# Attention scores with three persistent 32 KB buffers, and the second unit's transposes placed beside the third and fourth output tiles

## The chip, the cores and the metric

One core of a Trainium2 chip runs the kernel. The metric is the device time of one execution in microseconds; the runs of one kernel in one set of rounds lie within 0.1 to 0.5% of each other. A profiled execution gives the profile and the trace; its span (201.3 us for the kernel before) is about 1.8 us shorter than the device time.

## The reference

```python
batch, heads, seq, dim = 8, 8, 512, 64          # q, k: float32, 8.4 MB each
scale = 1.0 / np.sqrt(q.shape[-1])
return (np.einsum('bhqd,bhkd->bhqk', q, k) * scale).astype(np.float32)   # 67.1 MB
```

Two inputs are read once (16.8 MB together) and 67.1 MB are written: 83.9 MB cross the DMA engines whatever the order of work.

## The kernel before

The work is cut into 4 units of two batches. A unit is loaded as one 32 KB-per-partition tile (keys, then queries), cast to bf16 by POOL, transposed 128x128 at a time on PE, and copied out of PSUM into `kT` and `qz`. Then 4 output tiles of 4.19 MB are made per unit: 8 evacuations of PSUM each, and one store. The same pool of three 32 KB buffers serves the loads and the output tiles.

```python
big_pool = ctx.enter_context(tc.tile_pool(name="big", bufs=3))
# ...
def evacuate(dst, src):
    nonlocal n_evac
    if n_evac % 6 in (0, 2, 3):
        pinned(nc.scalar.mul(out=dst, in_=src, mul=scale))
    else:
        pinned(nc.vector.tensor_scalar(out=dst, in0=src, scalar1=scale, ...))
    n_evac += 1
# ...
def load_and_cast(v):
    xf = big_pool.tile([P, 2, 2, J * D], f32, name="big")
    for x, src in enumerate((k_r, q_r)):
        nc.sync.dma_start(out=xf[:, x], in_=...)
    for x in range(2):
        xb = bf_pool.tile([P, J, 2, D], bf16, name="xb")
        for s in range(2):
            pinned(nc.gpsimd.tensor_copy(out=xb[:, :, s, :], in_=xf[:, x, s]...))
# ... transpose(v, kb, qb): a generator of 40 steps; 8 groups of 8 transposes,
#     each group with 4 copies out of PSUM, on DVE and ACT in turn
def scores(v, t):
    o = big_pool.tile([P, 2, RO, S], f32, name="big")
    # ... 8 times: 2 matmuls into ps, evacuate(o[...], ps), yield
    nc.sync.dma_start(out=out_r[v, t], in_=o...)
# ...
for _ in transpose(0, *cast[0]):
    pass
for v in range(UNITS):
    ahead = transpose(v + 1, *cast[v + 1]) if v + 1 < UNITS else iter(())
    for t in range(TILES):
        for n, _ in enumerate(scores(v, t)):
            take(ahead, 1 + (t > 0 if v == 0 else n % 4 == 3))
```

`cast` is filled for all 4 units before the loop, so the fourth load waits for the first buffer, the first output tile for the second, and so on in rotation.

Of the kernel before, what the change touches and what calls it, by code (L numbers as in the profile page):

```python
# [1 line left out]

# [5 lines left out]


@with_exitstack  # L10
def kernel(
    ctx: ExitStack,
    tc: tile.TileContext,
    q: bass.AP,
    k: bass.AP,
    out: bass.AP,
):






    nc = tc.nc
    B, H, S, D = q.shape
    scale = 1.0 / (D ** 0.5)
    P = 128
    UNITS = B // 2
    N = H
    M = P // (2 * H)  # L30
    R = S // M
    J = R // 2
    RO = 8
    U = S // RO
    JJ = J // RO
    IW = 8 // JJ
    TILES = N // 2

    f32 = mybir.dt.float32
    bf16 = mybir.dt.bfloat16  # L40

    q_r = q.rearrange("(v b) g (m j) d -> v (b g m) (j d)", b=2, j=R)
    k_r = k.rearrange("(v b) g (m j) d -> v (b g m) (j d)", b=2, j=R)
    out_r = out.rearrange("(v b) (t x h) (u i) k -> v (b t) (h u) x (i k)", b=2, x=2, h=2, i=RO)

    consts = ctx.enter_context(tc.tile_pool(name="consts", bufs=1))

    big_pool = ctx.enter_context(tc.tile_pool(name="big", bufs=3))
    bf_pool = ctx.enter_context(tc.tile_pool(name="bf", bufs=6))
    t_pool = ctx.enter_context(tc.tile_pool(name="t", bufs=2))  # L50
    tpsum_pool = ctx.enter_context(tc.tile_pool(name="tpsum", bufs=2, space=bass.MemoryType.PSUM))
    psum_pool = ctx.enter_context(tc.tile_pool(name="psum", bufs=3, space=bass.MemoryType.PSUM))


    pinned = tc.keep_in_program_order

    n_evac = 0
    n_tp = 0

    def evacuate(dst, src):  # L60
        nonlocal n_evac

        if n_evac % 6 in (0, 2, 3):
            pinned(nc.scalar.mul(out=dst, in_=src, mul=scale))  # L64
        else:
            pinned(nc.vector.tensor_scalar(out=dst, in0=src, scalar1=scale, scalar2=None,  # L66
                                           op0=mybir.AluOpType.mult))
        n_evac += 1

    def half(h):  # L70
        return slice(h * D, (h + 1) * D)

    def load_and_cast(v):

        xf = big_pool.tile([P, 2, 2, J * D], f32, name="big")
        both = []
        for x, src in enumerate((k_r, q_r)):
            nc.sync.dma_start(out=xf[:, x], in_=src[v].rearrange("p (s c) -> p s c", s=2))  # L78
        for x in range(2):
            xb = bf_pool.tile([P, J, 2, D], bf16, name="xb")  # L80
            for s in range(2):
                pinned(nc.gpsimd.tensor_copy(out=xb[:, :, s, :],  # L82
                                             in_=xf[:, x, s].rearrange("p (j d) -> p j d", j=J)))
            both.append(xb)
        return both

    def rearrange(tp, pattern, dst):

        nonlocal n_tp
        copy = (nc.vector.tensor_copy, nc.scalar.copy)[n_tp % 2]  # L90
        n_tp += 1
        for s in range(2):
            src = tp[half(s)].rearrange(pattern, n=N, h=2)
            for h in range(2):
                pinned(copy(out=dst(s, h), in_=src[:, h]))  # L95
                yield

    def transpose(v, kb, qb):


        kT = t_pool.tile([P, N, M, 2, J], bf16, name="kT")
        qz = qzs[v % 2]
        ts[v] = (kT, qz)
        for j0 in range(0, J, 8):
            tp = tpsum_pool.tile([P, 8, P], bf16, name="tp")
            for j in range(8):
                pinned(nc.tensor.transpose(out=tp[:, j, :], identity=identity,  # L107
                                           in_=kb[:, j0 + j].rearrange("p s d -> p (s d)")))
            yield
            yield from rearrange(tp, "d j (n h m) -> d h n m j",  # L110
                                 lambda s, h: kT[half(h), :, :, s, j0:j0 + 8])
        for i0 in range(0, RO, IW):
            tp = tpsum_pool.tile([P, IW, JJ, P], bf16, name="tp")
            for i in range(IW):
                for jj in range(JJ):
                    pinned(nc.tensor.transpose(out=tp[:, i, jj, :], identity=identity,  # L116
                                               in_=qb[:, RO * jj + i0 + i].rearrange("p s d -> p (s d)")))
            yield
            yield from rearrange(tp, "d i jj (n h m) -> d h i n m jj",
                                 lambda s, h: qz[half(h), i0:i0 + IW, :, h * U:(h + 1) * U]  # L120
                                 .rearrange("d i n (m s jj) -> d s i n m jj", s=2, jj=JJ)[:, s])

    def scores(v, t):

        kT, qz = ts[v]
        o = big_pool.tile([P, 2, RO, S], f32, name="big")
        for x in range(2):
            n = 2 * t + x
            for i in range(0, RO, 2):
                ps = psum_pool.tile([P, 2, S], f32, name="ps")  # L130
                for w in range(2):
                    pinned(nc.tensor.matmul(out=ps[:, w, :], lhsT=qz[:, i + w, n, :],  # L132
                                            rhs=kT[:, n].rearrange("d m s j -> d (m s j)"),
                                            start=True, stop=True))
                evacuate(o[:, x, i:i + 2, :], ps)
                yield
        nc.sync.dma_start(out=out_r[v, t], in_=o.rearrange("p x i k -> p x (i k)"))  # L137

    def take(steps, count):
        for _ in range(count):  # L140
            next(steps, None)

    identity = consts.tile([P, P], dtype=bf16)
    make_identity(nc, identity)
    qzs = [consts.tile([P, RO, N, P], bf16, name=f"qz{n}") for n in range(2)]
    for qz in qzs:
        nc.vector.memset(qz, 0.0)  # L147
    cast = [load_and_cast(v) for v in range(UNITS)]

    ts = {}  # L150
# [4 lines that stand above are left out]
        for t in range(TILES):  # L155
            for n, _ in enumerate(scores(v, t)):

                take(ahead, 1 + (t > 0 if v == 0 else n % 4 == 3))
        for _ in ahead:
            pass  # L160


# [1 line left out]
_INS = ['q', 'k']  # L164
_OUTS = [((8, 8, 512, 512), 'float32')]


# [23 lines left out]
```

## Time and profile before

| | kernel before |
|---|---|
| time, median of 3 (low to high) | 203.24 us (202.83 to 203.37) |
| span of the profiled run | 201.3 us |
| busy: DMA queue / DVE / ACT / PE / POOL | 98.1% / 63% / 50% / 49% / 15% |
| moved over the span | 417 GB/s |
| stores 1, 2, 3, 4 issued at | 38.2, 46.0, 58.3, 63.6 us |
| least time from a store's issue to its landing | 15.8 us |

How to read it: the DMA row of the page is the mean busy share of 16 DMA engines in each fortieth of the span. The stage table has one line for each stretch, with the busy time of each engine and, in its last two columns, the DMA share and GB/s. "To landing" is counted from the issue on SP's queue to the completion that other engines can wait for. The prediction shows these lines.

### The profile page before, as it was taken

Reading aid. Unit: us, or ns where it says so; the run is one execution under the profiler, and the core shown is the slowest. Engines: PE = TensorE matmul, PEld = TensorE weight load, DVE = VectorE, ACT = ScalarE, POOL = GpSimd, SP = SyncE. Lnnn points to the kernel's source line nnn. Section 1 sums busy time; section 2 is a strip of 40 time slices with the busy share of each in tenths; the row PEclk is TensorE's granted clock in tenths of the full one; section 3 lists DMA queues with packets and bytes.
Section 4 is the critical chain, followed back from the end, with each engine's and each line's share of the span. In section 5 each row is a group of like instructions: output and inputs, shape, how many; then the busy total and the mean of one; then the engine's idle time right before and its main releaser. Section 6 shows DMA issues by size and latency. Waiting matters only on the chain.

```text
span 201.3 us, 1456 instructions
## 1 busy us (share of the span) xinstructions
PE 99.2 (49%) x503; PEld 48.3 (24%) x512; DVE 126.4 (63%) x130; ACT 100.7 (50%) x129; POOL 30.6 (15%) x22
## 2 busy tenths in 40 slices
PE   0033366753976729463729554856535666710000
PEld 0033353321522414231315221432212222200000
DVE  6726659995989929796749796569635264530000
ACT  2016667786674856583837663856515341510000
POOL 1277777556000000000000000000000000000000
PEclk9999999998599996999975998888995857555555
DMA  6999999999999999999999999999999999999993
GB/s 205 430 443 430 420 433 440 420 407 427 433 436 425 422 443 427 430 423 440 430 423 433 433 430 427 440 430 423 433 436 430 410 446 433 420 423 433 433 427 163
DMA packets 5510, 83.97 MB, mean 417 GB/s; under 512 B 384, under 2 KB 384, under 8 KB 384
## 3 DMA queue, kind: packets, MB, share of 16 engines
q1 hardware_dynamic: 5504, 83.89, 98.1%
q8 instruction: 4, 0.07, 0.1%
q14 instruction: 2, 0.02, 0.0%
HBM read 16.78 MB, written 67.11 MB: 417 GB/s over the span
## 4 chain that ended last, share of the span: by engine, by line
DMA 63%; DVE 16%; PE 3%; POOL 3%; ACT 1%; POOLq 1%; issue 1%; SPq 0%; DVEq 0%; ACTq 0%
DMA out_dram<-big 43%; DMA big<-in_q_dram 20%; DVE big L66 12%; PE ps L132 3%; DVE qz L95 3%; POOL xb L82 3%; DVE kT L95 1%; ACT big L64 1%; POOLq L186 1%; SPq L78 0%; DVEq L66 0%; SPq L137 0%; ACTq L64 0%; POOLq L82 0%
## 5 line engine op out<-in xcount | busy, mean ns | idle before, releaser
L132 PE MATMUL ps<-kT,qz 128*128 128x512 bf16 x247 | 81.1, 450 | 55.1 <-ACT big L64 39.2
L66 DVE TENSOR_SCALAR big<-ps 128x1024 f32<-128x1024 f32 x64 | 76.3, 1222 | 39.9 <-DMA out_dram<-big 29.1
L64 ACT ACTIVATE big<-ps 128x1024 f32<-128x1024 f32 x64 | 63.7, 1023 | 57.0 <-DMA out_dram<-big 30.8
L132 PEld LDWEIGHTS <-qz 128*128 128x128 bf16 x256 | 27.5, 111 | 96.0 <-issue 83.2
L82 POOL CAST xb<-big 128x2048 bf16<-128x2048 f32 x16 | 29.9, 1896 | 17.6 <-DMA big<-in_k_dram 11.9
L95 DVE COPY kT<-tp 64x512 bf16<-64x512 bf16 x32 | 22.0, 687 | 6.3 <-PE tp L107 5.7
L95 ACT COPY kT<-tp 64x512 bf16<-64x512 bf16 x32 | 18.5, 578 | 14.7 <-PE tp L107 14.4
L95 DVE COPY qz<-tp 64x512 bf16<-64x512 bf16 x32 | 22.0, 687 | 3.1 <-PE tp L116 2.7
L95 ACT COPY qz<-tp 64x512 bf16<-64x512 bf16 x32 | 18.5, 578 | 3.9 <-PE tp L116 3.6
L107 PE MATMUL tp<-identity,xb 128*128 128x128 bf16 x128 | 12.0, 254 | 16.5 <-POOL xb L82 12.5
L116 PE MATMUL tp<-identity,xb 128*128 128x128 bf16 x128 | 12.8, 265 | 6.0 <-DVE kT L95 3.5
L107 PEld LDWEIGHTS <-xb 128*128 128x128 bf16 x128 | 10.5, 116 | 20.8 <-POOL xb L82 12.8
L116 PEld LDWEIGHTS <-xb 128*128 128x128 bf16 x128 | 11.3, 122 | 10.9 <-issue 8.9
L147 DVE MEMSET qz<- 128x4096 uint32 x2 | 6.9, 3472 | 2.5 <-PEq L175 1.7
L95 ACT ACT_TABLE_LOAD x1 | 1.3, 1283 | 0.7 <-PEq L175 0.7
masks.py:199 POOL TENSOR_SCALAR_AFFINE_SELECT identity<-identity 128x128 bf16<-128x128 bf16 x1 | 0.3, 294 | 0.1
masks.py:197 POOL MEMSET identity<- 128x128 bf16 x1 | 0.2, 205 | 0.3 <-POOLq L175 0.3
L175 POOL MEMSET const-float32-0.0<- 128x1 f32 x1 | 0.1, 99 | 0.2 <-issue 0.2
L175 POOL MEMSET const-bfloat16-1.0<- 128x1 bf16 x1 | 0.1, 102 | 0.0
L175 POOL MEMSET const-uint8-127<- 128x1 uint8 x1 | 0.1, 102 | 0.0
L175 POOL MEMSET const-float32-1.0<- 128x1 f32 x1 | 0.1, 99 | 0.0
## 6 DMA issues: line engine op xcount, KB each, us to landing
out_dram<-big SPq DMA_DIRECT2D x16, 4096.0 KB, 21.4
big<-in_k_dram SPq DMA_DIRECT2D x4, 2048.0 KB, 19.2
big<-in_q_dram SPq DMA_DIRECT2D x4, 2048.0 KB, 24.2
```

Source lines behind the costliest of these rows:

```text
L64: pinned(nc.scalar.mul(out=dst, in_=src, mul=scale))
L66: pinned(nc.vector.tensor_scalar(out=dst, in0=src, scalar1=scale, scalar2=None, op0=mybir.AluOpType.mult))
L82: pinned(nc.gpsimd.tensor_copy(out=xb[:, :, s, :], in_=xf[:, x, s].rearrange("p (j d) -> p j d", j=J)))
L95: pinned(copy(out=dst(s, h), in_=src[:, h]))
L107: pinned(nc.tensor.transpose(out=tp[:, j, :], identity=identity, in_=kb[:, j0 + j].rearrange("p s d -> p (s d)")))
L116: pinned(nc.tensor.transpose(out=tp[:, i, jj, :], identity=identity, in_=qb[:, RO * jj + i0 + i].rearrange("p s d -> p (s d)")))
L132: pinned(nc.tensor.matmul(out=ps[:, w, :], lhsT=qz[:, i + w, n, :], rhs=kT[:, n].rearrange("d m s j -> d (m s j)"), start=True, stop=True))
L147: nc.vector.memset(qz, 0.0)
L175: nc = _bacc.Bacc("TRN2", target_bir_lowering=False, num_devices=1)
L186: with _tile.TileContext(nc) as tc:
```

## The change

The intent is to get the first stores out earlier: buffers that never go back to a pool are waited for part by part (the third tile's first evacuation starts at 41.2 us in the changed kernel, after the first cast of the fourth keys, and at 48.8 in the kernel before, after the last cast of that load); the first unit's transposes use all PSUM buffers and its first cast is shared between DVE and POOL; and the second unit's transposes no longer slow the first two output tiles but go beside the third and fourth. ACT takes two thirds of the evacuations instead of half.

```diff
-    big_pool = ctx.enter_context(tc.tile_pool(name="big", bufs=3))
...
-        if n_evac % 6 in (0, 2, 3):
+        if n_evac % 3 < 2:
             pinned(nc.scalar.mul(out=dst, in_=src, mul=scale))
...
+    def next_big():
+        nonlocal n_big
+        n_big += 1
+        return bigs[(n_big - 1) % 3]
...
-        xf = big_pool.tile([P, 2, 2, J * D], f32, name="big")
+        xf = next_big().rearrange("p (x s c) -> p x s c", x=2, s=2)
...
-                pinned(nc.gpsimd.tensor_copy(out=xb[:, :, s, :], in_=...))
+                copy = nc.vector.tensor_copy if v == x == s == 0 else nc.gpsimd.tensor_copy
+                pinned(copy(out=xb[:, :, s, :], in_=...))
...
+            if v == 0 and n_tp % 4 > 1:
+                tp = psum_pool.tile([P, W, P], bf16, name="ps")
+            else:
+                tp = tpsum_pool.tile([P, W, P], bf16, name="tp")
...
-        o = big_pool.tile([P, 2, RO, S], f32, name="big")
+        o = next_big().rearrange("p (x i k) -> p x i k", x=2, i=RO)
...
+    bigs = [consts.tile([P, 2 * RO * S], f32, name=f"big{n}") for n in range(3)]
...
-                take(ahead, 1 + (t > 0 if v == 0 else n % 4 == 3))
+                take(ahead, (0, 0, 3, 2)[t] if v == 0 else 1 + (n % 4 == 3))
```

More of the change, by code (lines that the diff above doesn't have):

```diff
@@ L35 @@
     JJ = J // RO
-    IW = 8 // JJ
     TILES = N // 2
@@ L46 @@
     consts = ctx.enter_context(tc.tile_pool(name="consts", bufs=1))
-    big_pool = ctx.enter_context(tc.tile_pool(name="big", bufs=3))
     bf_pool = ctx.enter_context(tc.tile_pool(name="bf", bufs=6))
     t_pool = ctx.enter_context(tc.tile_pool(name="t", bufs=2))
+    psum_pool = ctx.enter_context(tc.tile_pool(name="psum", bufs=3, space=bass.MemoryType.PSUM))
     tpsum_pool = ctx.enter_context(tc.tile_pool(name="tpsum", bufs=2, space=bass.MemoryType.PSUM))
-    psum_pool = ctx.enter_context(tc.tile_pool(name="psum", bufs=3, space=bass.MemoryType.PSUM))
     pinned = tc.keep_in_program_order
@@ L71, in half @@
         return slice(h * D, (h + 1) * D)
+    n_big = 0
+    def next_big():
+        nonlocal n_big
+        n_big += 1
+        return bigs[(n_big - 1) % 3]
     def load_and_cast(v):
-        xf = big_pool.tile([P, 2, 2, J * D], f32, name="big")
+        xf = next_big().rearrange("p (x s c) -> p x s c", x=2, s=2)
         both = []
@@ L81, in load_and_cast @@
             for s in range(2):
-                pinned(nc.gpsimd.tensor_copy(out=xb[:, :, s, :],
-                                             in_=xf[:, x, s].rearrange("p (j d) -> p j d", j=J)))
+                copy = nc.vector.tensor_copy if v == x == s == 0 else nc.gpsimd.tensor_copy
+                pinned(copy(out=xb[:, :, s, :], in_=xf[:, x, s].rearrange("p (j d) -> p j d", j=J)))
             both.append(xb)
@@ L103, in transpose, with transposed @@
         ts[v] = (kT, qz)
-        for j0 in range(0, J, 8):
-            tp = tpsum_pool.tile([P, 8, P], bf16, name="tp")
-            for j in range(8):
-                pinned(nc.tensor.transpose(out=tp[:, j, :], identity=identity,
-                                           in_=kb[:, j0 + j].rearrange("p s d -> p (s d)")))
+        W = 8
+        def transposed(rows):
+            if v == 0 and n_tp % 4 > 1:
+                tp = psum_pool.tile([P, W, P], bf16, name="ps")
+            else:
+                tp = tpsum_pool.tile([P, W, P], bf16, name="tp")
+            for w, row in enumerate(rows):
+                pinned(nc.tensor.transpose(out=tp[:, w, :], identity=identity,
+                                           in_=row.rearrange("p s d -> p (s d)")))
+            return tp
+        for j0 in range(0, J, W):
+            tp = transposed([kb[:, j0 + j] for j in range(W)])
             yield
             yield from rearrange(tp, "d j (n h m) -> d h n m j",
-                                 lambda s, h: kT[half(h), :, :, s, j0:j0 + 8])
+                                 lambda s, h: kT[half(h), :, :, s, j0:j0 + W])
+        IW = W // JJ
         for i0 in range(0, RO, IW):
-            tp = tpsum_pool.tile([P, IW, JJ, P], bf16, name="tp")
-            for i in range(IW):
-                for jj in range(JJ):
-                    pinned(nc.tensor.transpose(out=tp[:, i, jj, :], identity=identity,
-                                               in_=qb[:, RO * jj + i0 + i].rearrange("p s d -> p (s d)")))
+            tp = transposed([qb[:, RO * jj + i0 + i] for i in range(IW) for jj in range(JJ)])
             yield
-            yield from rearrange(tp, "d i jj (n h m) -> d h i n m jj",
+            yield from rearrange(tp.rearrange("p (i jj) c -> p i jj c", jj=JJ),
+                                 "d i jj (n h m) -> d h i n m jj",
                                  lambda s, h: qz[half(h), i0:i0 + IW, :, h * U:(h + 1) * U]
```

## The prediction

DVE's busy time came to about 101 us with a term for the first cast; without the term it is 126 - 22 x 1.2 = 99.6 us.

> **What bounds the kernel now.** I read the page's slices and DMA queue first, then a table of the DMA engines by stage, then how long a store takes from issue to landing, then the chain of work that ended last. First the page: the first line is the mean busy share of the 16 DMA engines in 40 slices, the second what they moved, then the queue, its share of the 16 engines' span, and the bytes.
>
> ```profile
> DMA  6999999999999999999999999999999999999993
> GB/s 205 430 443 430 420 433 440 420 407 427 433 436 425 422 443 427 430 423 440 430 423 433 433 430 427 440 430 423 433 436 430 410 446 433 420 423 433 433 427 163
> ...
> q1 hardware_dynamic: 5504, 83.89, 98.1%
> ...
> HBM read 16.78 MB, written 67.11 MB: 417 GB/s over the span
> ```
>
> Only the first and last of 40 slices are not full. The queue's packets cover 98.1% of a span of 201.3 us, so all idle time of the DMA engines together is 1.9% of it, 3.8 us. No compute engine comes near (DVE 63%, ACT 50%, PE 49%). The same by stage; the last two columns are the DMA share and GB/s:
>
> ```profile
> 0.00:4.00 4.00, 0.00 (x0) 0.00 (x0) 2.34 (x1) 1.28 (x1) 0.70 (x6) 1.00 0.57 147
> 4.00:30.00 26.00, 8.69 (x74) 7.56 (x76) 15.62 (x18) 9.87 (x17) 16.68 (x9) 1.00 1.01 431
> 30.00:46.00 16.00, 10.69 (x74) 5.49 (x73) 15.13 (x17) 12.79 (x18) 10.40 (x7) 1.00 1.01 422
> 46.00:64.00 18.00, 12.09 (x58) 5.73 (x57) 14.95 (x17) 11.38 (x16) 2.80 (x2) 0.81 1.01 432
> 64.00:150.00 86.00, 50.86 (x262) 23.88 (x266) 64.05 (x68) 53.50 (x68) 0.00 (x0) 0.90 1.01 430
> 150.00:197.00 47.00, 16.91 (x41) 5.60 (x41) 14.33 (x12) 11.85 (x12) 0.00 (x0) 0.58 1.01 430
> 197.00:201.25 4.25, 0.00 (x0) 0.00 (x0) 0.00 (x0) 0.00 (x0) 0.00 (x0) 0.50 0.25 108
> ```
>
> From 4 to 197 us the share is 1.01 in every stage, that is, full, at 422 to 432 GB/s: the stage of loads alone, the one in which loads give way to stores, and the stage of stores. What is lost is lost in the first 4 us (0.57 full, before the queue has filled) and the last 4.25 us (0.25, the engines finishing one after another). The time is therefore 83.9 MB / 430 GB/s = 195.1 us plus about 6.2 us of ramp and tail.
>
> How near was the queue to running dry? Each of the 16 stores moves 4.19 MB, alone 4.19 / 430 = 9.75 us. From issue to landing they took:
>
> ```profile
> DMA to landing us min/median/max: 15.8/21.4/23.4
> ```
>
> Even the quickest took 15.8 us, so at least about 15.8 - 9.75 = 6 us of other traffic was ahead of it at its issue. The timeline names that quickest store, the third, and the evacuation into the same buffer that its landing released:
>
> ```profile
> 58.31 0.37 SPq L137 DMA_DIRECT2D out_dram<-big  x1
> ...
> 74.21 1.02 ACT L64 ACTIVATE big<-ps 128x1024 f32<-128x1024 f32 x1 [1.84 <-DMA out_dram<-big]
> ```
>
> 74.2 - 58.3 = 15.9 us. So the tightest place of the whole kernel, where the changed code works, still had 6 us in hand. The chain in order of time looks different at that very place:
>
> ```profile
> 45.07 1.90 POOL xb L82
> 46.96 1.85 POOLq L186
> 48.84 1.23 DVE big L66
> ...
> 60.06 3.50 DVE big L66 x3
> 63.61 20.21 DMA out_dram<-big
> ```
>
> It walks through casts, copies and evacuations from 45 to 63.6 us and reads as if compute set the end. But the 20.21 us behind it is longer than the store's own 9.75 us: the store queued. While those engines are named, the DMA engines are full, so shortening this stretch only lengthens the queue.
>
> [...] Here it is the engines: a store's issue takes 0.37 us of SP, 16 of them about 6 us of 201. [...]
>
> **The change part by part.** Bytes, number and shape of the DMAs, and rotation of three buffers in one order, all stay as they were. The order of instructions built from both versions shows the 8 loads and 16 stores equal, and 128 score evacuations, 64 + 64 transpose copies and 16 casts in both.
>
> Persistent buffers. Before, the first evacuation into a re-used buffer waits for all loads and casts of it; in the changed build it waits for the part that it overwrites (one load and its own cast for each half of a tile). Third tile: before, its first evacuation starts at 48.8 us, when the last cast of the fourth load ends. After, its first half needs only the casts of the fourth key load (39.09 + 3.74 = 42.8 us), its second half those that end at 48.8. Worth up to about 6 us to that tile, off the DMA path.
>
> First cast on VectorE. Two casts of 1.87 us stood in a row on POOL (8.71 to 12.4). Now one runs on DVE after the second memset (5.93 + 3.47 = 9.4 us)[...].
>
> Four PSUM buffers for the first 8 groups of transposes. PE no longer waits for copies (the 2.44 and 2.36 us gaps). But the queries land at 13.5 and their casts end at 17.3 as before. From there: about 1.1 us of transposes, then 8 DVE copies of 0.70 = 5.6 us, ends at 24.0; before, 29.0. A gain of 5 us, off the DMA path.
>
> Placement and split. The 40 steps of the next unit's transposes leave the first two tiles and go beside the third (24) and fourth (16). First tile: 8 evacuations, 6 on ACT at 1.03 = 6.2 us from 24 us, so its store goes out near 30 us, not 38.2. Second tile: its second half waits for casts that end at 33.15 + 3.74 = 36.9, so about 38.5, not 46.0. Third tile: about half of its 19 or 20 copies on each engine; ACT 5 x 1.03 + 10 x 0.58 = 11 us, DVE 3 x 1.23 + 10 x 0.69 = 10.6 us, between 42 and, with the cast that ends at 48.8, about 52 us, not 58.3. Fourth: waits for the first store's landing, near 53 us, then ACT 6 x 1.03 + 8 x 0.58 = 10.8 us: 64 us, as before (63.6).
>
> Is the queue ever dry? All loads and two stores are 25.2 MB, 58.5 us of DMA from an effective start near 3.2 us: full until 61.7. The third store arrives at 52, 10 us ahead (before 6 counted by landing, 3.4 counted this way). With it the queue is full until 71.5, and the fourth arrives at 64, 7 us ahead. Later tiles: ACT 5.33 x 1.03 + 5 x 0.58 = 8.4 us against 9.75 us of DMA for each tile, with two stores ahead. Over the kernel ACT goes from 101 to about 101 + 22 x 1.0 = 123 us[...].
>
> Sum on the path that sets the end: 0 us. Predicted 203.1 us.
>
> **The rivals.** (1) The earlier stores share the DMA engines with the last loads instead of lining up, the last casts come late, and the third tile leaves a hole. For it: the last load landed near 45.0 us, 5.9 us after the one before, where earlier ones came 4.9 apart, and the 30 to 46 us stage moved 422 GB/s, not 431. Against it: even the worst case, the last load landing when all committed traffic ends at 61.7, gives its store at about 61.7 + 3.7 + 2.5 = 68, a hole of 6 us: 209 us. (2) ACT, now with two thirds of the evacuations, becomes the bound beside the third and fourth tiles: it would need 7 us more than I count before anything shows; a hole of 1 to 3 us gives 204 to 206. (3) The chain of waits is right and compute from 45 to 63 us does set the end: then 6 us less, 197. Against it stands the full DMA row; 2% of 203.24 is 4.1 us, more than all 3.8 us of idle time there is, and that lies in ramp and tail, which the change leaves alone.
>
> **Range and chances.** The three runs before span 202.83 to 203.37. I give 202.3 to 204.2 for 8 in 10, a little wider upward because a hole can only cost. Faster by over 2%: 0.01; it would need a higher DMA rate. Slower by over 2%: 0.03, rivals 1 and 2 at their worst. Within 2%: 0.96.
>
> **What would show it.** Right: the DMA row full in all but the first and last slice, 417 GB/s over the span, the stages above at 1.00 or more; the first three stores issued near 30, 38 and 52 us; the least issue-to-landing time above 15.8 us, the median still near 21; ACT busier than DVE; longer idle waits of ACT and DVE on stores. Wrong: a slice between 46 and 75 us below 9, or a store that lands within about 10 us of its issue (the queue ran dry); last loads landing long after 45 us (rival 1); or a DMA rate away from 430 GB/s.

## The result, and the profile after

The changed kernel took 203.42 us (median of 4, 203.35 to 203.51), the kernel before 203.04 us in the same rounds (202.83 to 203.37): ratio 1.0017, 95% interval 1.0000 to 1.0035. A ratio here is the mean time of one kernel's fast runs over that of the other's of the same rounds, so not quite the ratio of the medians quoted.

The page of the changed kernel, the same rows as shown of before, ahead of them the busy times:

```profile
PE 106.2 (53%) x503; PEld 50.8 (25%) x512; DVE 102.6 (51%) x109; ACT 121.0 (60%) x151; POOL 30.4 (15%) x21
...
DMA  6999999999999999999999999999999999999993
...
q1 hardware_dynamic: 5504, 83.89, 98.0%
```

DVE and ACT changed places as counted, by some 20 us each, and the DMA row is digit for digit the same. By stage:

```profile
0.00:4.00 4.00, 0.00 (x0) 0.00 (x0) 2.34 (x1) 1.28 (x1) 0.70 (x6) 1.00 0.58 152
4.00:30.00 26.00, 13.18 (x82) 8.87 (x84) 19.15 (x21) 14.36 (x22) 16.57 (x8) 0.93 1.01 430
30.00:46.00 16.00, 9.26 (x49) 4.14 (x48) 8.34 (x9) 9.50 (x12) 10.10 (x7) 0.88 1.01 419
46.00:64.00 18.00, 12.78 (x73) 6.74 (x73) 12.30 (x15) 14.61 (x20) 3.06 (x2) 0.73 1.01 430
```

Compare the 30 to 46 us stage: DVE does 8.3 us of work there instead of 15.1, ACT 9.5 instead of 12.8, and the DMA engines move 419 GB/s instead of 422. The stores came out earlier all the same. The third tile's last evacuation on DVE, its store's issue, and the times of all stores from issue to landing:

```profile
52.73 1.23 DVE L63 TENSOR_SCALAR big<-ps 128x1024 f32<-128x1024 f32 x1 [2.12 <-PE ps L144]
```

```profile
54.03 0.37 SPq L149 DMA_DIRECT2D out_dram<-big  x1
```

```profile
DMA to landing us min/median/max: 19.9/22.1/26.4
```

| store | before, us | after, us | predicted, us |
|---|---|---|---|
| 1 | 38.2 | 30.8 | 30 |
| 2 | 46.0 | 38.2 | 38.5 |
| 3 | 58.3 | 54.0 | 52 |
| 4 | 63.6 | 64.2 | 64 |
| 16 | 178.2 | 178.4 | |

Seven microseconds won at the first store are gone at the fourth, which waits for the first store to land (its first evacuation starts at 55.0 us, after ACT had waited 3.13 us for that landing): that waits in the queue, not on compute. The chain of waits still runs through the same place, with other engines named in it, and again a 20 us store behind it:

```profile
45.32 1.91 POOL xb L88
...
63.12 1.03 ACT big L61
64.17 19.88 DMA out_dram<-big
```

### The profile page after: what moved, and what is told of

The parts are those of the page before. It is cut to its first block, busy times and chain, and to the rows that moved or that the text cites. A ratio compares the mean times of both kernels' runs of the same rounds, so it can differ in the third digit from the quotient of the medians.

```text
span 201.6 us, 1521 instructions
## 1 busy us (share of the span) xinstructions
PE 106.2 (53%) x503; PEld 50.8 (25%) x512; DVE 102.6 (51%) x109; ACT 121.0 (60%) x151; POOL 30.4 (15%) x21
## 4 chain that ended last, share of the span: by engine, by line
DMA 63%; ACT 10%; PE 7%; POOL 3%; issue 2%; DVE 2%; ACTq 1%; SPq 0%; POOLq 0%
DMA out_dram<-big 43%; DMA big<-in_q_dram 20%; ACT big L61 8%; PE ps L144 6%; POOL xb L88 3%; ACT qz L100 2%; PE tp L117 1%; DVE kT L100 1%; DVE big L63 1%; ACT kT L100 1%; ACTq L199 1%; SPq L83 0%; ACTq L61 0%; POOLq L88 0%
## 5 line engine op out<-in xcount | busy, mean ns | idle before, releaser
L144 PE MATMUL ps<-kT,qz 128*128 128x512 bf16 x247 | 86.7, 483 | 53.8 <-ACT big L61 45.7
L61 ACT ACTIVATE big<-ps 128x1024 f32<-128x1024 f32 x86 | 84.3, 1023 | 43.3 <-DMA out_dram<-big 23.5
L63 DVE TENSOR_SCALAR big<-ps 128x1024 f32<-128x1024 f32 x42 | 51.4, 1225 | 66.8 <-DMA out_dram<-big 41.0
L117 PE MATMUL tp<-identity,xb 128*128 128x128 bf16 x224 | 22.5, 263 | 17.1 <-POOL xb L88 13.7
L100 ACT COPY kT<-tp 64x512 bf16<-64x512 bf16 x28 | 16.2, 579 | 12.6 <-PE tp L117 12.2
L100 DVE COPY kT<-tp 64x512 bf16<-64x512 bf16 x28 | 19.2, 687 | 4.4 <-PE tp L117 4.0
L100 DVE COPY qz<-tp 64x512 bf16<-64x512 bf16 x28 | 19.2, 687 | 0.4
L117 PE MATMUL ps<-identity,xb 128*128 128x128 bf16 x32 | 3.8, 314 | 0.0
L100 DVE COPY kT<-ps 64x512 bf16<-64x512 bf16 x4 | 2.8, 689 | 0.1
L100 DVE COPY qz<-ps 64x512 bf16<-64x512 bf16 x4 | 2.8, 689 | 0.1
```

Source lines behind the costliest of these rows:

```text
L100: pinned(copy(out=dst(s, h), in_=src[:, h]))
L117: pinned(nc.tensor.transpose(out=tp[:, w, :], identity=identity, in_=row.rearrange("p s d -> p (s d)")))
L144: pinned(nc.tensor.matmul(out=ps[:, w, :], lhsT=qz[:, i + w, n, :], rhs=kT[:, n].rearrange("d m s j -> d (m s j)"), start=True, stop=True))
```

## The experiments

Theory D: the DMA queue is never dry, so an earlier store only waits longer in it; the change buys slack, not time. Rival C: the compute chain of 45 to 63 us sets the end. Rival F, formed later: the 1.7 us between the kernel and its transfers alone come with the packets that the queue list calls "instruction" ("fetches" in the recorded text). Twelve kernels ran.

### Spending the slack: four delays

The last evacuation of the third tile is repeated on DVE, which leaves the result as it was and should hold the third store back by about 1.22 us for each repeat. In both kernels that evacuation is DVE's.

```diff
-            pinned(nc.vector.tensor_scalar(out=dst, in0=src, ...))
+            for _ in range(1 + (K if n_evac == 23 else 0)):
+                pinned(nc.vector.tensor_scalar(out=dst, in0=src, ...))
```

The kernel before with 3 repeats:

> The kernel before, with the last evacuation of the third tile done 4 times instead of once on DVE: 3 x 1.22 = 3.7 us later for its store (62.0 us instead of 58.3). DMA theory (the queue was never dry; it would be at about 61.7 us by bytes, 64.4 by the landing less 9.75): 0 to 0.5 us, ratio 1.000 to 1.0025. Chain theory (the compute work from 45 to 63 us sets the end): 3.7 us, ratio 1.018.

Before with 10 repeats:

> The same with 10 repeats, 12.2 us: third store at about 70.5 us. DMA theory: the queue runs dry between 61.7 and 64.4 us and waits until 70.5: 6 to 9 us longer, ratio 1.030 to 1.044, and a slice near 62 to 70 us below 9 in the DMA row. Chain theory: 12.2 us, ratio 1.060.

The changed kernel with 5 repeats:

> The changed kernel, the last evacuation of the third tile done 6 times: 6.1 us later, third store at about 60.1 us instead of 54.0. DMA theory: still ahead of 61.7, so 0 us against the changed kernel, ratio to the kernel before 1.000 to 1.004. Chain theory: 6.1 us, ratio 1.03.

The changed kernel with 10 repeats:

> The same with 10 repeats, 12.2 us: third store at about 66.3 us. DMA theory: dry from 61.7 to 64.4 until 66.3: 2 to 4.6 us, and 4.3 us less than the kernel before pays for the same 10 repeats, which is how much earlier the third store had become; ratio 1.010 to 1.025. Chain theory: 12.2 us, ratio 1.06.

Measured, in the same rounds (kernel before 202.90 us):

| kernel | third store issued, us | time, us | ratio to before, 95% interval |
|---|---|---|---|
| before, 3 repeats | 61.0 | 204.03 | 1.0058 (1.0043 to 1.0073) |
| before, 10 repeats | 69.8 | 212.97 | 1.0504 (1.0479 to 1.0530) |
| changed, 5 repeats | 60.2 | 203.32 | 1.0022 (1.0007 to 1.0037) |
| changed, 10 repeats | 66.7 | 209.49 | 1.0324 (1.0306 to 1.0341) |

The same ten repeats, 12.2 us of DVE work, cost 10.1 us before (212.97 - 202.90) and 6.1 us in the changed kernel (209.49 less its own 203.42): 4.0 us less, where the third store had become 4.3 us earlier. And 6.1 us of delay cost the changed kernel nothing: 1.0022 is what it has without delay. Rival C wants each delay paid in full, in both kernels; it falls. So does the idea that nothing was gained: the change turned about 2 us of slack (12.2 - 10.1) into about 6 (12.2 - 6.1). These two are good to about 0.7 us: against the undelayed profiles the store moved by 11.5 us before (58.3 to 69.8) and 12.7 in the changed kernel (54.0 to 66.7), which gives 1.4 and 6.6 us, because the work ahead of the repeats is itself up to 1 us earlier or later from one profile to the next.

But both costs lie above what D expected, 6 to 9 and 2 to 4.6 us. The stages of the kernel before with 10 repeats show where the hole begins and ends:

```profile
58.00:60.00 2.00, 0.59 (x2) 0.19 (x2) 1.93 (x3) 1.28 (x2) 0.00 (x0) 1.00 1.07 459
60.00:62.00 2.00, 0.68 (x2) 0.19 (x2) 1.97 (x2) 0.00 (x0) 0.00 (x0) 0.60 0.50 213
62.00:64.00 2.00, 0.00 (x0) 0.00 (x0) 1.93 (x3) 0.00 (x0) 0.00 (x0) 0.50 0.02 8
64.00:66.00 2.00, 0.00 (x0) 0.00 (x0) 1.95 (x2) 0.00 (x0) 0.00 (x0) 0.50 0.00 0
...
70.00:72.00 2.00, 1.84 (x4) 0.40 (x3) 2.00 (x3) 0.01 (x1) 0.00 (x0) 0.50 0.77 328
```

The engines are half idle already in 60 to 62 us, so they finish at about 61.0 on the mean. The store is issued at 69.8, and the packet records of the trace have its first data packet at 70.7: the restart costs 0.9 us (as in the changed kernel with 10 repeats, 66.7 to 67.6). The idle shares add up to 1.0 + 2.0 + 3 x 2.0 + 0.5 = 9.4 us for one engine, and from 61.0 to 70.7 it is 9.7, near the 10.1 us measured. The queue is dry at 61, near the count by bytes (61.7), not at 64.4, as counted back from a landing. The engines do not end together: in this trace the last data packet before the hole ends at 62.9 us. And the restart comes on top. The count by bytes comes nearer still with the start read from the stage table: 147 GB/s in the first 4 us is 0.59 MB, or 1.4 us at 430 GB/s, so the transfers start in effect at 2.6 us, not 3.2, and 58.5 us later it is 61.1. That is also why 3 repeats, with the store at 61.0, cost 1.1 us where up to 0.5 was expected: in that run's trace the DMA share falls to 0.65 and 0.77 in the two microseconds from 61 to 63.

### The parts of the change

The changed kernel once more, unaltered:

> The changed kernel once more, unaltered, to settle the 0.3 us by which it came out slower. If that was the chip's scatter: ratio 0.9985 to 1.0015. If it is real: 1.001 to 1.003, with its place in the tail, since all stages before move the same GB/s.

It took 203.42 us, ratio 1.0019 (1.0006 to 1.0032). So the 0.3 us look real. They lie in the tail, as expected: in the packet records of the traces the last packet ends at 200.34 us in the changed kernel's profile and 200.39 in this run's, at 200.09 in the kernel before. Their cause is not settled. The data stages move nearly the same GB/s; the queue list of the changed kernel has one instruction packet more on q14 (3, not 2), and the trace gives such a packet (8 KB) 0.31 us. But the kernel before with persistent buffers has 4 of them at 1.0006 (0.9992 to 1.0019), so a simple count does not explain it.

The first cast back on POOL:

```diff
-                copy = nc.vector.tensor_copy if v == x == s == 0 else nc.gpsimd.tensor_copy
+                copy = nc.gpsimd.tensor_copy
```

In this expectation and the next, the name of a theory is cut: it named a mechanism that no run shows.

> The changed kernel with the first cast back on POOL. [...] (the DVE cast held POOL's own cast up): the POOL casts take 1.87 us each again, not 3.58, and the first transposes start near 12.4 us, 0.2 later than in the changed kernel, so the move to DVE had bought almost nothing. Rival (the 3.58 us come from elsewhere): the first POOL cast stays above 3 us and the transposes start near 14 us. Time the same on both, within 0.3 us of the changed kernel.

203.32 us, 1.0012 (1.0000 to 1.0025). First, the two casts of the changed kernel (POOL's and DVE's); then POOL's first cast in this run:

```profile
8.65 3.58 POOL L88 CAST xb<-big 128x2048 bf16<-128x2048 f32 x1 [7.35 <-DMA big<-in_k_dram]
...
9.32 1.16 DVE L88 CAST xb<-big 128x2048 bf16<-128x2048 f32 x1
```

```profile
8.61 1.89 POOL L88 CAST xb<-big 128x2048 bf16<-128x2048 f32 x1 [7.30 <-DMA big<-in_k_dram]
```

With DVE casting beside it, POOL's cast of the same size takes 3.58 us instead of 1.89. Two casts in a row on POOL end at about 12.3 us; one on each engine end at 12.2. The first transpose starts at 12.39 in this run and at 12.29 in the changed kernel: sharing the cast bought 0.1 us. That DVE's cast is what holds POOL's up is shown by taking it away: POOL loses 1.7 us to a cast of 1.16. By what means is not shown.

Both first casts on DVE:

```diff
-                copy = nc.vector.tensor_copy if v == x == s == 0 else nc.gpsimd.tensor_copy
+                copy = nc.vector.tensor_copy if v == x == 0 else nc.gpsimd.tensor_copy
```

> The changed kernel with both casts of the first keys on DVE, none on POOL at that time. [...] 2 x 1.16 us from 9.3, transposes start near 11.7 us, 0.6 before the changed kernel; the following POOL casts at 1.87. Time the same within 0.3 us, because the query casts (17.3 us) and the DMA queue set what follows.

203.25 us, 1.0011 (0.9999 to 1.0024). DVE takes 2.29 us for both from 9.32, the transposes start at 11.67, and POOL's following casts take 1.87 each. As expected, early keys get no one further: the first store goes out at 31.2 us, not earlier than 30.8.

The pool of three buffers in the changed kernel, nothing else undone:

```diff
+    big_pool = ctx.enter_context(tc.tile_pool(name="big", bufs=3))
...
-        return bigs[(n_big - 1) % 3]
+        return big_pool.tile([P, 2 * RO * S], f32, name="big")
```

> The changed kernel with the old pool of three buffers in place of the persistent ones, everything else as changed. First evacuation of the third tile waits for the last cast, 48.9 us, then about 11 us of ACT and DVE work: third store near 60 us, not 54. The delay runs put the latest harmless moment near 60.2 us, so 0 to 1.5 us over the changed kernel, ratio to before 1.001 to 1.009. If tracking by parts does not matter: third store still near 54 and no cost.

203.22 us, 1.0009 (0.9996 to 1.0023). The third store goes out at 59.5 us, the least issue-to-landing time is 14.0 us. The store is 5.4 us later than with persistent buffers, and later than in the kernel before: with the transposes beside the third tile, it is the start in part that keeps slack. The store is still just ahead of the dry queue (the DMA share dips to 0.84 from 61 to 62 us), so it costs nothing.

Persistent buffers alone, in the kernel before (the `next_big` lines of the change and nothing else):

> The kernel before with persistent buffers alone. First evacuation of the third tile from 41 us instead of 48.8; its copies (q transposes of the second unit) and last casts at 48.9 as before: third store near 53 us, not 58.3, least issue-to-landing time near 20 us. Time unchanged by the DMA theory: ratio 0.998 to 1.003. Chain theory: 3 to 5 us less, ratio 0.98.

203.01 us, 1.0006 (0.9992 to 1.0019). A miss in the mechanism: the third store goes out at 57.4 us, not 53, and the least issue-to-landing time is 14.4 us, not near 20. The tile's first evacuations start at 47.9 us, not 41, because DVE is busy until 47.8 with the second tile and the transposes beside it. The wait that persistent buffers take away was hidden behind the placement that the other part removes. Even the 0.9 us by which the third store is earlier than in the kernel before can't be put down to the buffers: in this profile the last load's casts start at 44.0 us instead of 45.1, and in the kernel before with 10 repeats, which has the old pool, they also start at 44.0 and the first evacuation at 47.8. So alone the buffers show no gain; with the other parts, 5.4 us.

### How far from the floor

The same 8 loads and 16 stores with no compute at all. Its output is wrong, which doesn't matter for the time.

```diff
-    # casts, transposes, scores, evacuations
+    o = consts.tile([P, 2, RO, S], f32, name="o")
+    nc.vector.memset(o, 0.0)
+    # 8 loads into 4 tiles, then 16 stores of o, without a wait on data
```

> Wrong on purpose: the same 8 loads and 16 stores, no compute, each store from one zeroed buffer, so no store waits for an evacuation. DMA theory: this is the floor, 201.5 to 203.5 us, ratio 0.99 to 1.002; the remaining time is ramp and tail. Chain theory: with the compute gone at least 6 us go too, 197 or less, ratio below 0.97.

201.22 us, ratio 0.9914 (0.9902 to 0.9927), a little below the expected range, far above what rival C wants. All compute together costs 1.7 us (202.94 - 201.22). They are in the tail. Bare transfers, from 196 us on (columns: DVE, POOL, clock, DMA share, GB/s):

```profile
196.00:197.00 1.00, 0.00 (x0) 0.00 (x0) 1.00 0.88 377
197.00:198.00 1.00, 0.00 (x0) 0.00 (x0) 1.00 0.62 262
198.00:199.00 1.00, 0.00 (x0) 0.00 (x0) 1.00 0.00 0
```

The kernel before, in the same microseconds:

```profile
197.00:198.00 1.00, 0.00 (x0) 0.00 (x0) 0.00 (x0) 0.00 (x0) 0.00 (x0) 0.50 0.69 295
198.00:199.00 1.00, 0.00 (x0) 0.00 (x0) 0.00 (x0) 0.00 (x0) 0.00 (x0) 0.50 0.31 131
199.00:200.00 1.00, 0.00 (x0) 0.00 (x0) 0.00 (x0) 0.00 (x0) 0.00 (x0) 0.50 0.08 33
```

Without compute all engines are done soon after 198 us (the last packet ends at 198.1); with it, most finish then and a few run on to 200. The bare run's queue list has no "instruction" packets; the kernel's has 4 of 16 KB on q8, and its trace gives them 0.88 to 1.10 us each, with a data packet of that size at 0.61. Hence rival F, tested by adding to the bare transfers only PE instructions (and the making of one constant tile) that depend on no transfer:

```diff
+    for _ in range(512):
+        nc.tensor.transpose(out=sink, in_=idle, identity=idle)
```

> Wrong on purpose: the bare transfers plus 512 transposes on PE that read one constant tile and depend on no transfer: the same 1026 PE rows as in the kernel, no other compute. Fetch theory (the 1.7 us between the bare transfers and the kernel are instruction fetches that ride on the same DMA engines, each holding one engine back about 0.9 to 1.1 us, so the last engine ends later): the queue list shows about 4 instruction packets on q8 and the time rises by 0.8 to 1.6 us over bare_dma, in the tail. Rival (data traffic of DVE, ACT and POOL, or waits of stores for buffers, make the tail): no rise, within 0.3 us of bare_dma.

202.96 us, ratio to before 1.0003 (0.9991 to 1.0015): the whole 1.7 us are back, a little more than expected. The two bare kernels ran in different rounds, each beside the kernel before; their ratios to it, 0.9914 and 1.0003, carry the comparison. Its queue list and its tail:

```profile
q1 hardware_dynamic: 5504, 83.89, 98.1%
q8 instruction: 4, 0.07, 0.1%
```

```profile
197.00:198.00 1.00, 0.00 (x0) 0.00 (x0) 0.00 (x0) 0.00 (x0) 0.50 0.77 328
198.00:199.00 1.00, 0.00 (x0) 0.00 (x0) 0.00 (x0) 0.00 (x0) 0.50 0.31 131
199.00:200.00 1.00, 0.00 (x0) 0.00 (x0) 0.00 (x0) 0.00 (x0) 0.50 0.08 33
```

This is the tail of the kernel before, made by PE instructions that read no transfer and that were over by 31.7 us. PE's work was there too, so the instruction packets are shown as its companions, not in isolation; but in the trace each of the 4 packets (0.97 to 1.01 us here) falls in a gap of an engine's data: on the mean 15.1 data packets are under way during it, 16.1 in the microsecond before. Why do packets of about 1 us move the end by 1.7? The packet records of the trace show most of it: the data packet that follows each of them takes 1.08 to 1.16 us instead of 0.61 (0.99 to 1.08 in the trace of the kernel before), so one costs its engine about 1.5 us. And four engines end late, at 199.4, 199.5, 199.9 and 200.0 us, the other twelve by 198.5: one late engine for each instruction packet, so no two need have met on one engine. Why the packet after it is long, and the last 0.2 us or so, stay open.

### An attempt on the ramp

The first three query loads from ACT's queue, beside SP's:

```diff
-            nc.sync.dma_start(out=xf[:, x], in_=...)
+            queue = nc.scalar if x == 1 and v < 3 else nc.sync
+            queue.dma_start(out=xf[:, x], in_=...)
```

> The changed kernel with the first three query loads issued from ACT's queue beside SP's: an attempt on the ramp, the only idle time besides the tail. DMA theory: at most the 0.4 to 1 us that issuing in a row takes in the first 4 us, ratio 0.996 to 1.002; the order of landing may change (queries beside keys), which moves the first transposes later but not the end.

203.62 us, 1.0033 (1.0019 to 1.0047): not faster, and beyond its range. The first slice of the span does move 247 GB/s instead of 205, but between 40 and 44 us the engines move 324 instead of 385 GB/s (share 0.93 instead of 0.97), and the first store goes out at 34.5 us. Which of these makes the loss was not tested. No run pointed to a version that beats both kernels.

## Why the prediction was right

- The bound. It said that the DMA engines are full and that 2% is more than all their idle time. The delays show it (6.1 us of delay free in the changed kernel), and the bare transfers bound the possible gain with these 24 transfers at 0.9%.
- The sum of zero on the path that sets the end: measured +0.3 us, ratio 1.0017 and again 1.0019. That small rise was not foreseen and is not explained.
- The stores at 30, 38.5, 52 and 64 us came at 30.8, 38.2, 54.0 and 64.2. The third was 2 us off: the working counts copies on ACT and DVE alone, and DVE's last evacuation of that tile waited 2.12 us for PE. Its sum is also loose: from 42.8, when it has the tile start, 11 us of work ends at 53.8, not 52 (the tile started at 41.2).
- The gain forecast from the cast on DVE failed: the first transposes start at 12.29 instead of 12.49 us, only 0.2 us sooner. DVE's cast took 1.16 us, but POOL's cast beside it became 1.7 us longer, which the working did not have.
- "The tightest place of the whole kernel ... still had 6 us in hand" was mis-sized. It took the landing time less the transfer for slack. The delays put it near 2 us; the count by bytes in the same text, 3.4 us, was closer: it had the start of the transfers 0.6 us too late and left out the restart. Dry at 61.0, less the store at 58.3, less 0.9 for the restart, is 1.8. The comparison of the two kernels held: 4 to 5 us more slack.
- Persistent buffers, "worth up to about 6 us to that tile": 5.4 us beside the other parts, nothing that can be told alone. The step was right in company and wrong for the buffers by themselves.
- Rival 1 (stores delaying the last loads) made no hole: in the changed kernel the last load's cast starts at 45.3 us, 45.1 before, though the first store was issued 7.4 us sooner. A small part of it may be there: in the three variants of the kernel before whose first store left at 38.9 us or later, the cast starts at 44.0; with the old pool in the changed kernel, first store at 33.6, it is 44.4. No run tested that. The prediction's "earlier ones came 4.9 apart" misses that the seventh load too came 5.9 us after the sixth (casts at 33.15 and 39.09 us). Rival 2 (ACT as the bound) did not come with 60% busy.
- The ramp and tail, called something "which the change leaves alone", were left alone; what goes with 1.7 us of the tail was found only afterwards.

## What to carry to other kernels

When the DMA row is full from ramp to tail, as in both kernels here (first store 7.4 us sooner, time 0.3 us longer), read every gain elsewhere as slack, and measure the slack by spending it: a repeated instruction that delays one store shows in two runs how much is there. Estimate it beforehand in bytes already issued, less the restart (here 1.8 us, with 0.9 for the restart, where the delays found about 2), not by how long a transfer took to land (6 us). Test the parts of a change together as well as alone, since one part's wait may be hidden behind what another part removes.
